# Low parts of a projection's weights on VectorE instead of GpSimd, in a hybrid attention and DeltaNet decoder step

## The chip, the core and the metric

The kernel runs on one core of a Trainium2 chip. The time is the device time of one execution in microseconds (us). Five engines work side by side, each through its own queue in order: TensorE (PE in the profile; its weight loads are PEld), VectorE (DVE), ScalarE (ACT), GpSimd (POOL) and SyncE (SP), which issues all DMA transfers here. An instruction that waits holds up all that stands behind it on its engine.

## The reference, cut to what matters

One layer of a decoder, for 1024 prompt tokens and 8 single-token samples, all in fp32:

```python
h = rms_norm(x, norm_mix_pre)
proj = h @ w_in                     # 1024 -> 2824 columns: q k v of attention, q k v z a b of DeltaNet
attn_o = window_attend(...)         # 8 heads, window 128, sinks, ALiBi
gdn_o  = gdn_chunked(...)           # 4 heads: conv, l2 norms, triangular inverse, scan over chunks
x = x + rms_norm(concat(attn_o, rms_norm(gdn_o) * silu(z)) @ w_out, norm_mix_post)
h = rms_norm(x, norm_ffn_pre)
x = x + rms_norm(relu(h @ w_up) ** 2 @ w_down, norm_ffn_post)
```

## The kernel before, in words

The tokens are worked in two halves, A (tokens 0 to 511 and the 8 samples) and B (512 to 1023). Every large product is made of three fp32r matmuls: an operand is split into a high part (a rounded copy, `wh` for weights, `h0h`, `h1h`, `xh` for activations) and a low part (the rest, `wl`, `h0l`, `h1l`, `xl`), and high times high, high times low and low times high are added up in PSUM.

The weights come in units: a block of 128 columns with 1024 rows, 512 KB. `w_dma` loads unit i into `wr` two units ahead, and `w_chain` splits it one unit ahead: ScalarE copies `wr` to `wh`, and then `wl = wr - wh` is made by VectorE or by GpSimd, or half by each. `wr`, `wh` and `wl` have two buffers each, so a unit can be split only when the unit two before it is done with. Unit 0 holds the two gate columns (a, b), units 1 to 22 the projections of half A, 23 the gates again, 24 to 41 the first 18 projections of half B, 42 to 49 the output projection `w_out` of half A, 50 to 53 the last four projections of half B, and from 54 on come the feed-forward weights. For units of the kind "pool" the planner decides from its own costs who makes `wl`: GpSimd if it is seen free early enough, half each if later, VectorE if later still. Units of the kind "dve" are VectorE's. Unit 1 is always GpSimd's, unit 2 always VectorE's.

The order of all instructions is not written by hand. While the program is built, the planner (`_Sched`) runs one main stream, the large matmuls, and many side chains (convolutions, gates, norms, attention heads, DeltaNet heads) as generators against a small cost table, and puts a step of a chain between the matmuls when the table says that its inputs are there. So a change in what one step costs, or in the engine that does it, shifts the order of everything that follows on all engines, until the chains have run out.

Side chains that matter below: the gate chain (`gates`), some 30 tiny VectorE instructions on the tile `abT` that end in `gg`, which TensorE multiplies with a triangle of ones into `gps` and transposes in `gtp`. The DeltaNet chain of a head: transposes `kps` and `qps`, products `kkq`, `Am`, an inversion on VectorE (`W`, `Ab`, `TW`), a round trip through DRAM (`Zd`), and then `yps`, `Y`, `zps`, `ztp` in three levels, and the scan `xps`, `ups`, `so`. After `w_out` each of half A's token tiles gets its residual and its norm: the sums of squares go to GpSimd (`ssA`), VectorE makes `hy` (residual) and `xrA` (normalised), and TensorE transposes that in `trp`, before the feed-forward can begin (matmuls into `two`). At the very end `run_tail` finishes the last product token tile by token tile, and `evac` writes the squares into a spare PSUM bank (`sq`).

Of the kernel before, what the change touches and what calls it, by code (L numbers as in the profile page):

```python
# [15 lines left out]
P = 128  # L16
DM = 1024
KD = DM // P
# [24 lines left out]
TH1, TH2 = 6500.0, 4500.0  # L43
# [219 lines left out]
def _body(ctx, tc, I, C, O):  # L263
    nc = tc.nc
    sp = nc.sync
    S = _Sched()
# [67 lines left out]
    def f32(ap):  # L334
        return ap.bitcast(F32)
# [55 lines left out]
    units = []  # L391
# [25 lines left out]
    def w_chain(i):  # L417
        _, shape, eng = units[i]
        raw, _, _, t, ev = wt[i]
        t0 = S.t["pe"]  # L420
        S.cur = max(S.t["pe"], t)
        yield
        if shape[-1] == 8:

            hi, lo = wt[i][1], None
            if hi is None:
                hi = wst_tile()
            CP(hi[:, :, 0:8], raw, "pool")
            TT(hi[:, :, 8:16], raw, f32(hi[:, :, 0:8]), ALU.subtract, "pool")
        else:  # L430
            hi = wp.tile([P] + shape, F32R, tag="wh", name="wh")
            lo = wp.tile([P] + shape, F32R, tag="wl", name="wl")
            A(hi, raw)
            yield
            n = 0 if i == 1 else shape[0] if i == 2 else shape[0] if eng == "dve" or max(S.t["pool"], S.cur) + 2300.0 > t0 + TH1 else (
                shape[0] // 2 if max(S.t["pool"], S.cur) + 2300.0 > t0 + TH2 else 0)
            c0 = S.cur
            if n:
                TT(lo[:, :n], raw[:, :n], f32(hi[:, :n]), ALU.subtract)
            c0, S.cur = S.cur, c0  # L440
            if n < shape[0]:
                TT(lo[:, n:], raw[:, n:], f32(hi[:, n:]), ALU.subtract, "pool")
            S.cur = max(S.cur, c0)
        wt[i][1:3] = [hi, lo]
        S.signal(ev)
# [1073 lines left out]
    LATE = 4  # L1519
# [3 lines left out]
            return [QO + 64 * h, QO + 64 * (4 + h)]  # L1523
        return [{"k": GO + 512, "q": GO, "v": GO + 1024, "z": ZO, "K": KO, "V": VO}[kd] + (h * P if kd in "kqvz" else 0)]

    def units_proj(g, cols):
        if cols[0][1] == 0:
            units.append(([(slice(None), w_in[:, :, ABO:ABO + 8])], [KD, 8], None))
        for kd, h in cols:
            cc_ = unit_cols(kd, h)  # L1530
            w = P // len(cc_)
            units.append(([((slice(None), slice(None), slice(i * w, (i + 1) * w)), w_in[:, :, c:c + w])
                           for i, c in enumerate(cc_)], [KD, P], "pool"))

    w_out = I["w_out"][0]
    KORD = [4, 0, 1, 5, 6, 7, 2, 3]
# [28 lines left out]
    units_proj(0, proj_cols(0))  # L1565
    units_proj(1, proj_cols(1)[:-LATE])
    units_w()
    units_proj(1, proj_cols(1)[-LATE:])
    PLAIN = (8, 2)
    units_up(PLAIN[0])  # L1570
    after_up = [len(units)]
# [9 lines left out]
    def unit_begin():  # L1581

        i = st["u"]
        st["u"] += 1
        return i
# [579 lines left out]
    class Contract:  # L2165
# [107 lines left out]
        def run_tail(self, i, bank, acc, dh):  # L2273
            unit_begin()
            xs = []

            for t, ks in ((0, (0, 1)), (1, (0, 1)), (0, (2, 3)), (1, (2, 3)), (2, range(4)), (3, range(4))):
                c = slice(t * P, (t + 1) * P)
                for k in ks:
                    u, j = i + k // 2, k % 2  # L2280
                    if k == len(xs):
                        yield from w_wait(u)
                        xs.append((yield from self.part(len(self.seq) - 4 + k)))
                    xh, xl = xs[k]
                    for ci, (a, w) in enumerate(((xh, 1), (xh, 2), (xl, 1))):
                        MM(acc[t], a[:, c], wt[u][w][:, j, :], False, k == 3 and ci == 2)
                        yield
                if k == 3:
                    S.cur = S.t["pe"] + S.LAT["pe"]
                    for _ in evac(acc[t], bank[t], P, self.ys[t], self.ss, t, dh, self.w, B.tile(t, [P, 512], "sq")):  # L2290
                        pass

    def evac(ps, bank, n, y, ss, i, dh, w, sq=None):
# [154 lines left out]
```

## Time and profile before

| | |
|---|---|
| time, median of 3 runs | 1304.32 us (1301.70 to 1306.08) |
| profiled execution, time | 1301.07 us |
| its span, first to last instruction | 1299.3 us |
| mean granted TensorE clock over the span | 0.993 of full speed |
| PE busy | 1261.0 us, 97% of the span |
| DVE busy | 902.4 us, 69% |
| ACT busy | 683.5 us, 53% |
| POOL busy | 357.2 us, 27% |

The profiled execution lies 1.8 us longer than its span, and 3.25 us below the median of the three runs. "Busy" is the time in which an engine has an instruction under way, with its waits for a port inside. For PE it says nothing on the clock: a matmul at half the clock is busy twice as long.

### The profile page before, as it was taken

The page shows a single profiled execution, that of the slowest core. Times are in us where ns is not written, and L with a number is a line of the kernel's source. Part 1 is how long each engine was busy: PE and PEld are TensorE (multiplying, and loading weights), DVE is VectorE, ACT ScalarE, POOL GpSimd, SP SyncE. Part 2 cuts the span into 40 slices and gives each one's busy share as a digit, 9 for nine tenths or more (in the row PEclk, how much of TensorE's full clock was granted, in tenths as well). Part 3 has the DMA queues.
Part 4 walks back from the last instruction along what each step waited for, and adds up shares of the span by engine and source line. Part 5 has one row for each costly group of instructions (what it writes and reads, how often), then busy time and mean ns, then how long its engine had stood idle before and what let it go on. Part 6 is the DMA issues. An engine that isn't in the chain of part 4 may idle for free.

```text
span 1299.3 us, 22677 instructions
## 1 busy us (share of the span) xinstructions
PE 1261.0 (97%) x8624; PEld 1081.0 (83%) x8624; DVE 902.4 (69%) x1708; ACT 683.5 (53%) x1409; POOL 357.2 (27%) x367
## 2 busy tenths in 40 slices
PE   8899999999999998999999999999998999999998
PEld 7898998777777776899999877777788999988886
DVE  5649878878777777678895479454478988544555
ACT  5466555645654545656665455343346666444442
POOL 4354344342253355103232330000034432000001
PEclk9899999999999998999999999999999999999999
DMA  6443325263233353133432443224345433243332
GB/s 184 131 118 100 79 66 139 75 149 89 65 100 94 94 159 119 51 112 105 114 111 98 130 162 99 81 82 149 93 121 155 119 100 103 92 162 98 97 98 98
DMA packets 199165, 142.57 MB, mean 110 GB/s; under 512 B 39406, under 2 KB 171822, under 8 KB 199032
## 3 DMA queue, kind: packets, MB, share of 16 engines
q1 hardware_dynamic: 199056, 141.12, 37.3%
q8 instruction: 68, 1.11, 0.4%
q14 instruction: 41, 0.34, 0.1%
HBM read 126.39 MB, written 15.85 MB: 109 GB/s over the span
## 4 chain that ended last, share of the span: by engine, by line
PE 84%; DVE 11%; ACT 2%; issue 1%; DMA 1%; POOL 1%; SPq 0%; DVEq 0%; POOLq 0%; ACTq 0%
PE acc L275 33%; PE ups L275 22%; PE pps L275 14%; PE dacc L275 2%; PE two L275 1%; DVE W L294 1%; PE so L275 1%; DVE kq L299 1%; PE kkq L275 1%; PE zps L275 1%; PE yps L275 1%; PE trp L282 1%; PE oa L275 1%; PE sps L275 1%; PE pps L282 1%
## 5 line engine op out<-in xcount | busy, mean ns | idle before, releaser
L275 PE MATMUL acc<-wh,xh 128*128 128x512 f32 x624 | 248.6, 398 | 0.0
L275 PE MATMUL acc<-wl,xh 128*128 128x512 f32 x624 | 245.0, 393 | 0.0
L275 PE MATMUL acc<-wh,xl 128*128 128x512 f32 x624 | 244.5, 392 | 0.1
L286 ACT ACTIVATE wh<-wr 128x1024 fp32r<-128x1024 f32 x161 | 169.2, 1051 | 67.1 <-PE pps L275 29.4
L294 DVE TENSOR_TENSOR xl<-u,xh 128x512 fp32r<-128x512 f32 x124 | 85.8, 692 | 143.1 <-ACT xh L286 143.1
L286 ACT ACTIVATE xh<-u 128x512 fp32r<-128x512 f32 x124 | 78.3, 631 | 191.7 <-PE acc L275 191.6
L294 POOL TENSOR_TENSOR wl<-wr,wh 128x1024 fp32r<-128x1024 f32 (+1 forms) x57 | 128.0, 2246 | 183.3 <-ACT wh L286 180.3
L294 DVE TENSOR_TENSOR wl<-wr,wh 128x1024 fp32r<-128x1024 f32 (+1 forms) x118 | 152.2, 1291 | 34.5 <-ACT wh L286 34.1
L275 PEld LDWEIGHTS acc<-wh,xh 128*128 128x128 f32 x624 | 117.1, 188 | 38.2 <-ACT xh L286 11.9
L275 PEld LDWEIGHTS acc<-wh,xl 128*128 128x128 f32 x624 | 117.2, 188 | 25.5 <-DVE xl L294 1.4
L294 POOL TENSOR_TENSOR st<-wr 128x512 f32<-128x512 f32 x54 | 85.4, 1588 | 189.5 <-DVE sl L294 84.0
L275 PEld LDWEIGHTS acc<-wl,xh 128*128 128x128 f32 x624 | 117.2, 188 | 22.8 <-DVE wl L294 0.2
L275 PE MATMUL ups<-T,sh 128*128 128x256 f32 (+1 forms) x648 | 120.6, 282 | 0.0
L275 PEld LDWEIGHTS ups<-T,sh 128*128 128x128 f32 x648 | 101.3, 188 | 0.0
L286 ACT ACTIVATE u<-u 128x520 f32<-128x520 f32 (+3 forms) x118 | 68.7, 582 | 53.8 <-DVE u L294 53.0
L275 PE MATMUL ups<-T,sl 128*128 128x256 f32 (+1 forms) x324 | 91.1, 281 | 0.3 <-DVE sl L294 0.3
L275 PE MATMUL ups<-h1h,wl 128*128 128x256 f32 (+2 forms) x328 | 86.5, 288 | 1.3 <-DVE wl L294 1.3
L275 PE MATMUL ups<-h1h,wh 128*128 128x256 f32 (+2 forms) x328 | 86.8, 288 | 0.0
L275 PE MATMUL ups<-h1l,wh 128*128 128x256 f32 (+2 forms) x328 | 86.6, 288 | 0.0
L275 PE MATMUL pps<-h1h,wl 128*128 128x512 f32 x176 | 73.1, 415 | 0.3 <-DVE wl L294 0.3
L275 PE MATMUL pps<-h1h,wh 128*128 128x512 f32 x176 | 72.0, 409 | 0.5 <-ACT acc L286 0.5
L275 PE MATMUL pps<-h1l,wh 128*128 128x512 f32 x176 | 72.1, 410 | 0.0
(403 smaller groups left out, 2876.8 us busy)
## 6 DMA issues: line engine op xcount, KB each, us to landing
wr<-in_w_up SPq DMA_DIRECT2D x64, 512.0 KB
wr<-in_w_down SPq DMA_DIRECT2D x64, 512.0 KB
wr<-in_w_in SPq DMA_DIRECT2D x36, 512.0 KB
wr<-in_w_in SPq DMA_DIRECT2D x16, 256.0 KB
wr<-in_w_out SPq DMA_DIRECT2D x16, 256.0 KB
wr<-in_w_out SPq DMA_DIRECT2D x32, 128.0 KB
xf<-x1d SPq DMA_DIRECT2D x8, 512.0 KB
xa<-in_x_prompt SPq DMA_DIRECT2D x4, 512.0 KB
```

The source lines that it names most:

```text
L275: ins = nc.tensor.matmul(out, lhsT=lhsT, rhs=rhs, start=start, stop=stop, **kw)
L282: ins = nc.tensor.transpose(out, in_, idn)
L286: ins = nc.scalar.activation(out, in_, func, **kw)
L294: ins = _e(eng).tensor_tensor(out=out, in0=a, in1=b, op=op)
L299: ins = nc.vector.scalar_tensor_tensor(out=out, in0=a, scalar=s, in1=b, op0=op0, op1=op1)
```

## The change

Three edits. The units with an index below 7, whose kind was "pool", get the kind "dve" (the special case of unit 2 goes away with that, and unit 1 stays with GpSimd). The last four projections of half B get the kind "dve" as well. In `run_tail` the squares of the third token tile go into bank 3 instead of 2, those of the fourth into bank 0 instead of 3.

```diff
@@ w_chain
-            n = 0 if i == 1 else shape[0] if i == 2 else shape[0] if eng == "dve" or max(S.t["pool"], S.cur) + 2300.0 > t0 + TH1 else (
+            n = 0 if i == 1 else shape[0] if eng == "dve" or max(S.t["pool"], S.cur) + 2300.0 > t0 + TH1 else (
                 shape[0] // 2 if max(S.t["pool"], S.cur) + 2300.0 > t0 + TH2 else 0)
@@
-    def units_proj(g, cols):
+    def units_proj(g, cols, eng="pool"):
...
-                           for i, c in enumerate(cc_)], [KD, P], "pool"))
+                           for i, c in enumerate(cc_)], [KD, P], "dve" if len(units) < 7 else eng))
...
-    units_proj(1, proj_cols(1)[-LATE:])
+    units_proj(1, proj_cols(1)[-LATE:], "dve")
@@ run_tail
-                    for _ in evac(acc[t], bank[t], P, self.ys[t], self.ss, t, dh, self.w, B.tile(t, [P, 512], "sq")):
+                    for _ in evac(acc[t], bank[t], P, self.ys[t], self.ss, t, dh, self.w, B.tile((0, 1, 3, 0)[t], [P, 512], "sq")):
```

The planner then makes another order on all five engines. Over the whole program the low part of 43 whole units and 14 half units was GpSimd's; now it is 34 whole and 16 half ones. TensorE's order is the same in its first 190 rows and again from row 2487 of 6798 on, which is the beginning of the feed-forward of half A. The two places below show how it shifts.

On VectorE, early in the projections of half A, this piece of the difference shows the low part of unit 3 coming in. `abT` rows belong to the gate chain and `kq` rows to the first convolution.

```order
 L294 TENSOR_TENSOR abT<-abT 128x5x4
 L308 TENSOR_SCALAR abT<-AB 128x5x4
+L294 TENSOR_TENSOR wl<-wr,wh 128x1024
 L299 SCALAR_TENSOR_TENSOR kq<-ext,cw,kq 128x4x128
 L306 TENSOR_SCALAR abT<-abT 128x5x4 x2
```

The low parts of units 4, 5 and 6 come in further on in the same way (those of 4 and 5 ahead of `gg`, that of 6 behind it), and three more rows of convolutions now stand ahead of `gg`: nine instead of six.

On TensorE, the place of `gps`, which needs `gg`. Before, it stands in the matmuls of unit 4 (`wh_475`, into `pps_557` and `pps_558`), four pairs after their start:

```order
L275 MATMUL pps_557<-h0h0_137,wl_476 128x256
L275 MATMUL pps_558<-h0h0_137,wl_476 128x264
L275 MATMUL pps_557<-h0h0_137,wh_475 128x256
L275 MATMUL pps_558<-h0h0_137,wh_475 128x264
L275 MATMUL gps_575<-gg_102,cst_sb_93 128x16
L275 MATMUL pps_557<-h0l0_139,wh_475 128x256
```

Now it stands at the end of unit 4, where unit 5 (`wh_551`) begins:

```order
L275 MATMUL pps_547<-h0h1_138,wl_476 128x256
L275 MATMUL pps_548<-h0h1_138,wl_476 128x264
L275 MATMUL gps_623<-gg_102,cst_sb_93 128x16
L275 MATMUL pps_629<-h0h0_137,wh_551 128x256
L275 MATMUL pps_630<-h0h0_137,wh_551 128x264
```

Counted from the first matmul of unit 2, `gps` came after 104 matmuls before and comes after 144 now.

On TensorE, in the last four projections of half B (units 50 to 53, 96 matmuls of 128x512 into `pps`), the first level of the last DeltaNet head. Before, it stands in the third of the four, after 71 of the 96 matmuls:

```order
L275 MATMUL pps_5708<-h1l1_902,wh_5644 128x512
L275 MATMUL yps_5773<-W_5109,Am1_5367 64x32 x8
L275 MATMUL pps_5708<-h1h1_900,wl_5645 128x512
L275 MATMUL pps_5790<-h1h0_899,wh_5710 128x512
L275 MATMUL pps_5790<-h1l0_901,wh_5710 128x512
L275 MATMUL zps_5796<-Y1_5772,T1_5730 64x32 x8
L275 MATMUL ztp_5797<-T1_5730,Y1_5772 64x32 x8
L275 MATMUL pps_5790<-h1h0_899,wl_5711 128x512
```

Now all 96 come first (`pps_5766` is the fourth projection), then the transposes of the normalised tokens with some attention scores (`sps`), and the head's first level behind them, with no large matmul between its steps:

```order
L275 MATMUL pps_5766<-h1h1_892,wl_5729 128x512
L282 MATMUL trp_5822<-ident_60,xrA_5582 128x128 x4
L282 MATMUL trp_5828<-ident_60,xrA_5582 128x128 x4
L282 MATMUL trp_5834<-ident_60,xrA_5582 128x128 x4
L275 MATMUL sps_5854<-KT_97,mix1_2044 128x256
L275 MATMUL sps_5855<-KT_97,mix1_2044 128x256
L282 MATMUL trp_5889<-ident_60,xrA_5582 128x128 x4
L275 MATMUL yps_5896<-W_5170,Am1_5417 64x32 x8
L275 MATMUL zps_5915<-Y1_5895,T1_5872 64x32 x8
L275 MATMUL ztp_5916<-T1_5872,Y1_5895 64x32 x8
L282 MATMUL trp_5937<-ident_60,xrA_5582 128x128 x4
L275 MATMUL two_5953<-h1h0_5815,wh_5768 128x256
```

On VectorE the end of that head's inversion (the copy of `TW` that goes to DRAM) now stands right behind the `xrA` of the third token tile; before, it stood ahead of the residual of the second tile.

## Rows read from the trace of the kernel before

**Rows 1.** Stretches: length; PE, PEld, DVE, ACT, POOL busy us (instructions); clock, DMA, GB/s
```profile
0.00:555.00 555.00, 529.29 (x4068) 444.73 (x4069) 407.63 (x1053) 302.17 (x764) 224.87 (x255) 0.99 0.39 106
555.00:1299.30 744.30, 731.68 (x4558) 636.29 (x4557) 494.75 (x656) 381.29 (x646) 132.38 (x112) 1.00 0.37 112
0.00:20.00 20.00, 14.47 (x69) 10.74 (x70) 10.48 (x22) 12.60 (x26) 10.46 (x25) 1.00 0.82 229
```

**Rows 2.** Waits of PE: who for whom, us in total, times, longest
```profile
PE zps L275 <- DVE Y L294: 4.2, 1, 4.2
PE gps L275 <- DVE gg L299: 3.9, 1, 3.9
```

**Rows 3.** Busy times (PE, PEld, DVE, ACT, POOL) and clock around `gps`
```profile
27.60:39.84 12.24, 12.24 (x105) 12.24 (x103) 9.74 (x26) 5.58 (x10) 6.30 (x8) 1.00 0.76 213
39.84:44.12 4.28, 0.40 (x5) 0.19 (x3) 4.18 (x9) 0.85 (x3) 2.67 (x3) 0.89 0.03 9
44.12:49.90 5.78, 5.78 (x26) 5.71 (x27) 3.83 (x7) 1.35 (x3) 0.00 (x0) 0.50 0.05 13
```

**Rows 4.** Busy times and clock in the last four projections of half B
```profile
473.00:497.00 24.00, 20.22 (x107) 15.58 (x106) 20.68 (x23) 12.23 (x23) 18.90 (x22) 1.00 0.79 246
492.00:505.00 13.00, 7.13 (x64) 5.53 (x63) 11.59 (x14) 5.57 (x11) 10.92 (x13) 0.74 0.54 169
```

**Rows 5.** Timeline of PE there: start, duration, operation, [idle before it]
```profile
473.68 0.50 PE L275 MATMUL pps<-h1h,wh 128*128 128x512 f32 x1 [0.52 <-ACT acc L286]
...
493.91 0.66 PE L275 MATMUL yps<-W,Am 64*64 64x32 f32 x16 [1.71 <-DMA W<-Zd]
...
499.61 1.06 PE L275 MATMUL zps<-Y,T 64*64 64x32 f32 x16 [4.15 <-DVE Y L294]
...
512.59 1.97 PE L282 MATMUL trp<-ident,xrA 128*128 128x128 f32 x16
...
517.15 2.10 PE L275 MATMUL sps<-KT,mix 64*128 64x256 f32 x16
```

**Rows 6.** Timeline of POOL (start, duration, operation, [idle before it]), one of three such
```profile
34.45 2.40 POOL L294 TENSOR_TENSOR wl<-wr,wh 128x1024 fp32r<-128x1024 f32 x1 [2.23 <-ACT wh L286]
```

**Rows 7.** Timeline of DVE ahead of `gps`
```profile
29.77 2.40 DVE L299 SCALAR_TENSOR_TENSOR kq<-ext,cw,kq 128x512 f32<-128x512 f32 x1 [2.06 <-ACT kq L286]
32.69 0.65 DVE L299 SCALAR_TENSOR_TENSOR kq<-ext,cw,kq 128x512 f32<-128x512 f32 x1
...
34.50 2.38 DVE L294 TENSOR_TENSOR abT<-abT 128x20 f32<-128x20 f32 x1
...
43.88 0.18 DVE L299 SCALAR_TENSOR_TENSOR gg<-abT,alg 128x20 f32<-128x20 f32 x1
```

**Rows 8.** Groups of the page: low parts on either engine, whole span
```profile
L294 POOL TENSOR_TENSOR wl<-wr,wh 128x1024 fp32r<-128x1024 f32 (+1 forms) x57 | 128.0, 2246 | 183.3 <-ACT wh L286 180.3
L294 DVE TENSOR_TENSOR wl<-wr,wh 128x1024 fp32r<-128x1024 f32 (+1 forms) x118 | 152.2, 1291 | 34.5 <-ACT wh L286 34.1
```

**Rows 9.** Timeline of ACT, the high part of unit 5
```profile
39.08 1.06 ACT L286 ACTIVATE wh<-wr 128x1024 fp32r<-128x1024 f32 x1 [3.02 <-PE pps L275]
```

**Rows 10.** Timeline of POOL in the last four projections of half B
```profile
495.13 2.35 POOL L294 TENSOR_TENSOR wl<-wr,wh 128x1024 fp32r<-128x1024 f32 x1
```

**Rows 11.** Timeline of DVE in the last four projections of half B
```profile
477.98 1.78 DVE L294 TENSOR_TENSOR wl<-wr,wh 128x512 fp32r<-128x512 f32 x1
...
495.20 3.35 DVE L299 SCALAR_TENSOR_TENSOR hy<-hy,ssA,xrA 128x1024 f32<-128x1024 f32 x1 [0.72 <-POOL ssA L294]
...
499.66 1.28 DVE L299 SCALAR_TENSOR_TENSOR xrA<-hy,ssA 128x1024 f32<-128x1024 f32 x1
```

**Rows 12.** Timeline of an earlier head: end of its inversion, its `yps`
```profile
383.08 0.67 DVE L323 TENSOR_REDUCE TW<-W 32x64 f32<-32x512 f32 x1
...
390.61 0.66 PE L275 MATMUL yps<-W,Am 64*64 64x32 f32 x16 [0.36 <-DMA W<-Zd]
```

**Rows 13.** Timeline of ACT in the tail, squares of the third token tile
```profile
1290.20 0.58 ACT L286 ACTIVATE sq<-acc 128x512 f32<-128x512 f32 x1 [2.03 <-PE acc L275]
```

## The prediction

> **What bounds the kernel now.** I read the busy times by stretch first. TensorE is busy for 529.3 of the first 555 us and for 731.7 of the other 744.3 [rows 1], and its order from the feed-forward of half A on is unchanged, so what the change can win or lose lies in the first 555 us: 25.7 us of TensorE's idle time, and the matmuls that run at the lower clock. 5.5 us of that idle time is the start of the kernel [rows 1], ahead of all that changes. The waits of TensorE [rows 2] name the two longest, 3.9 us before `gps` and 4.2 us before `zps`, and each is a single wait. They lie at the two places that the change touches; call them A (us 40 to 50) and B (us 492 to 505).
>
> At A TensorE is full and at full clock until 39.84, then it works 0.40 of 4.28 us, and the next 5.78 us run at a granted clock of 0.50, which is 1.2 GHz of 2.4 [rows 3]. So A costs 3.88 us of waiting and half of 5.78, 2.9 us, together 6.8. At B TensorE works 7.13 of 13 us at a mean clock of 0.74 [rows 4]: 5.87 us idle, which is the 1.71 before `yps` and the 4.15 before `zps` [rows 5], and 13 x 0.26 / 0.5 = 6.8 us at the lower level, part of them idle. At most half of 6.8 is lost to it, 3.4; I take 2 as my estimate. B costs about 8. The rest, 25.7 - 5.5 - 3.9 - 5.9 = 10.4 us, is spread over 500 us in waits of which none is as long.
>
> **Place A.** The reader should see why `gg` is late. While GpSimd makes a low part from 34.45 to 36.85 [rows 6], VectorE's `abT` instruction on 20 columns runs from 34.50 to 36.88 [rows 7]: it ends when GpSimd does. The first tap `kq` takes 2.40 us beside such a low part and 0.65 without [rows 7]. Three low parts fall into this chain, so they cost VectorE about 1.75 + 2.2 + 2.2 = 6.1 us, and the planner's table has no such cost. With the change these low parts are VectorE's own, at no more than the 1.29 us mean of its group [rows 8]: three of them ahead of `gg`, 3.9 us. Three more convolution rows stand ahead of it, 3 x 0.65 = 2.0. `gg`, which ended at 43.88 + 0.18 = 44.06 [rows 7], would end at 44.06 - 6.1 + 3.9 + 2.0 = 43.9. VectorE must also wait for the high parts in this order; that of unit 5 is done at 39.08 + 1.06 = 40.1 [rows 9], and by my sum VectorE gets there at about the same time, so I allow 0.5 more: 44.4.
>
> TensorE used to stand at `gps` at 40.24. The new place is 40 matmuls later, 0.117 us each (105 in 12.24, [rows 3]), 4.7 us: 44.9. So `gg` should be there with half a microsecond to spare, the wait goes, and with it the fall of the clock, which came after it. Cover for the low parts themselves: the low part of unit 5 is done at 40.1 + 1.29 = 41.4 and needed at 44.9; if VectorE were more than 3.5 us later than that, each microsecond more would be one of TensorE's. A short wait at `gtp` may be left, since one convolution row now lies between `gps` and the copy that `gtp` reads. Gain at A: between 3.9 (the clock still falls, 2.9 lost again) and 6.8; I take 6.5, since the cause is removed and not moved.
>
> The Trainium skill has a rule on this (SBUF — State Buffer, Who interferes with whom): a VectorE instruction with two SBUF inputs and a GpSimd instruction that reads SBUF cannot run together, and the later one is blocked for the whole of the other. The trace agrees, 2.38 us for a 20-column instruction. But another page of the Trainium skill, Perfetto Trace Analysis, Optimizing Scalar/DVE Operations, says that moving work between these two engines might not help for that reason, and taken alone that speaks against the change. By it VectorE is taken for about as long either way, and the sum would be zero.
>
> **Place B.** Here the reader should compare what is late. GpSimd's low part at 495.13 [rows 10] lies beside the residual `hy` of 3.35 us at 495.20, against 1.28 for the same size [rows 11]; I found one more such pair, so 2 x 2.07 = 4.1 us of VectorE go. In their place come four whole low parts, 4 x 1.29 = 5.2, less the 1.78 of the half one that VectorE already made there [rows 11], so 3.4 more. The start of the inversion of the last head, about 2.3 us of small instructions by my estimate, now also falls into this stretch. Before, the `xrA` of the third token tile ended at 499.66 + 1.28 = 500.94 [rows 11], 27.3 us after the first of the 96 matmuls at 473.68 [rows 5]. Now: 27.3 + 3.4 + 2.3 - 4.1 = 28.9 if VectorE had no other slack; but it had 24 - 20.68 = 3.3 us idle [rows 4], some of it in waits for GpSimd, so 25.6 to 28.9. Middle: 27.
>
> TensorE: before, the 71 matmuls up to `yps` and four small groups of transposes took 493.91 - 473.68 - 1.71 = 18.5 us [rows 5], 0.26 each; 96 take 25.0, and two transposes of 0.49 (1.97 for four, [rows 5]) 1.0. It then waits for the third tile from 26 to 27. From there to `yps` it has five transposes, 2.5, and a group of scores, half of 2.10 [rows 5]: 3.5 us. But `yps` needs the round trip through DRAM, and at an earlier head it took 390.61 - (383.08 + 0.67) = 6.9 us from the last reduction to `yps` [rows 12]. That reduction, 0.7 us, now stands right behind the third `xrA`, so `yps` waits 0.7 + 6.9 - 3.5 = 4.1 us, with nothing left to put before it. `zps` follows with no large matmul between and waits for `Y`, one small VectorE instruction and the way there and back; I estimate 0.9, and 2 if VectorE is behind. Sum: 1 + 4.1 + 0.9 = 6.0 idle, against 5.87 before, and a clock that falls again for about as long. So B is exchanged for itself: 0, with bounds from +3 (third tile at once, clock stays up) to -4 (third tile 2 us later still, `Y` late, clock lost 3.4).
>
> **The tail.** The squares of the third token tile begin at 1290.20 [rows 13], and the trace puts the idle time before them to the last matmul of that tile alone; no bank held them up. The fourth writes into a bank that nobody reads. I cost this edit at 0; a matmul, not the bank, is the cover.
>
> **The middle.** From A to B the order of some 2,000 rows is shuffled. GpSimd has nine whole low parts less (2.25 us mean of all forms, [rows 8]) and VectorE nine more; the planner knows what a low part costs on VectorE and not what it costs beside GpSimd, so its places should be no worse. I count 0, with 4 us either way out of the 10.4 that wait there.
>
> **Sum.** 6.5 + 0 + 0 + 0. Against the profiled execution, 1301.07 - 6.5 = 1294.6. The median of the runs lies 3.25 above that execution, so the prediction is 1304.32 - 6.5 = 1297.8 us.
>
> **The rivals.** A difference of 0.3%, 3.9 us, is about what a measurement of this kernel can tell from none.
>
> First, A goes and B shrinks too: VectorE delivers the third tile on time and the shuffle is kind. 6.8 + 3 + up to 4 gives 1304.3 - 13.8 = 1290.5. For it speaks that GpSimd's sums of squares no longer stand behind its low parts; against it the round trip, which no engine's speed shortens. Chance 0.19.
>
> Second, the wait only moves: A's gain is eaten by a new wait in the shuffled middle, one of 3 to 4 us, as two already are, with the clock down behind it. 6.5 - 4 - 2 leaves about 1304, within 0.3%. For it speaks that VectorE, the busier of the two (407.6 against 224.9 us of 555, [rows 1]), takes on more. The sentence of the Trainium skill against moving work between the two (Perfetto Trace Analysis, Optimizing Scalar/DVE Operations) would end here too. Chance 0.24.
>
> Third, slower: VectorE becomes the bound at B. TensorE's loss there is then the wait for the third tile, 4.1 before `yps`, 2 before `zps`, and 4 to 5 to the clock. If the tile came 36 us after the first of the 96 matmuls instead of 27, that is 10 + 4.1 + 2 + 4.5 = 20.6 against 8 before: 12.6 lost, less A's 6.5, 1304.3 + 6 = 1310. It eats A's gain from about 30 us on and makes the kernel measurably slower from 34, or from 31 if A keeps its slow clock and gains 3.9 alone. For it speaks that VectorE is busy 20.68 of 24 us there [rows 4]; against it that a fifth of this is time at the port, which goes. Chance 0.12.
>
> **How the numbers follow.** My forecast, A gone and B exchanged, has 0.45, and with the first rival faster has 0.64; same 0.24, slower 0.12. The range takes in the first rival's 1290 and the upper end of no change: 1304.3 and the spread of the runs, 1306. Below and above lie about 0.2. The likeliest case's own range is 1294 to 1300.
>
> **What would show it.** In the profile after: no wait of TensorE before `gps`, and a full clock from us 40 to 50; no VectorE instruction of 2.4 us from 27 to 45. At B a wait before `yps` put down to the DMA of `W`, of about 4 us, and a short one before `zps`; the third tile's `trp` some 27 us after the first of the 96 matmuls. TensorE's idle time of the first 555 us near 22, and everything behind the first `ups` shifted as a block. The prediction is wrong if a new wait of over 3 us with a fall of the clock stands between A and B, or if the low parts of units 3 to 6 hold up TensorE themselves.

## The result, and the profile after

The changed kernel is slower: 1312.99 us (median of six runs, 1310.95 to 1317.48) against 1304.30 for the kernel before in the same comparison (six runs, 1300.94 to 1306.13). The ratio is 1.0074, with a 95% interval of 1.0055 to 1.0092. The profiled execution took 1312.95 us, its span 1311.2, its mean granted clock 0.988.

The time was not lost where the change was made. Starts of TensorE's first matmul at seven places, and the end of the span, from the two timelines (us):

| place in the program | before | after | difference |
|---|---|---|---|
| `gps` of half A (place A) | 44.12 | 44.35 | +0.2 |
| first projection of half B | 209.93 | 203.66 | -6.3 |
| `gps` of half B | 249.01 | 250.47 | +1.5 |
| second `dkr` (decode states) | 284.85 | 292.06 | +7.2 |
| first `acc` (`w_out` of half A) | 402.05 | 409.15 | +7.1 |
| first of the last four projections (place B) | 473.68 | 485.14 | +11.5 |
| first `two` (feed-forward of half A) | 516.50 | 522.35 | +5.9 |
| end of the span | 1299.3 | 1311.2 | +11.9 |

So A gave 6 us, as forecast. The stretch from half B's first projection to the second `dkr`, which the prediction counted as 0, cost 13.5. From the first `acc` on, B's 5.6 are mostly work brought forward: TensorE is busy 5.3 us longer in the stretch ahead of the last four projections (69.67 and 74.95 us) and 3.4 less in them (36.74 and 33.33), so the two together gained 1.3. TensorE's order is that of before again from us 554.8 before and 563.1 after. There the changed kernel is 8.3 us late, about what the medians differ by (8.7). The other 3.5 us of the 11.9 come behind that, nearly all at one `ups` of the feed-forward of half B, where two executions of one and the same order differ as well (see the experiment on SP below); the profiled execution of before lies 3.25 below its median and that of after on it.

Place A in the profile after, timeline of VectorE (start, duration, operation): a low part, a tap that took 2.40 us before [rows 7], and `gg`.

```profile
28.63 1.22 DVE L294 TENSOR_TENSOR wl<-wr,wh 128x1024 fp32r<-128x1024 f32 x1 [1.45 <-ACT wh L286]
29.77 0.74 DVE L299 SCALAR_TENSOR_TENSOR kq<-ext,cw,kq 128x512 f32<-128x512 f32 x1
...
42.84 0.18 DVE L299 SCALAR_TENSOR_TENSOR gg<-abT,alg 128x20 f32<-128x20 f32 x1
```

`gg` ends at 43.02 and `gps` starts at 44.35 with no wait. The waits of TensorE after (who for whom, us in total, times, longest) name what came instead; [rows 2] has those of before:

```profile
PE dkr L275 <- DMA S<-in_state_gdn: 4.8, 2, 4.2
PE gps L275 <- DVE gg L299: 3.7, 1, 3.7
...
PE xps L275 <- DVE S L299: 2.6, 2, 2.0
PE pps L275 <- DVE wl L294: 2.5, 3, 1.3
```

This `gps` is that of half B. Busy times by stretch after (length; PE, PEld, DVE, ACT, POOL busy; clock, DMA, GB/s), to be read beside [rows 1, 3]:

```profile
0.00:555.00 555.00, 523.89 (x3999) 438.36 (x4000) 406.43 (x1059) 298.25 (x755) 206.44 (x244) 0.98 0.39 105
40.00:49.90 9.90, 9.90 (x85) 9.88 (x84) 7.09 (x17) 3.52 (x8) 0.77 (x2) 1.00 0.35 76
200.00:240.00 40.00, 36.93 (x301) 28.27 (x300) 32.20 (x141) 20.49 (x70) 13.02 (x24) 0.96 0.43 112
240.00:260.00 20.00, 16.34 (x118) 12.74 (x117) 16.39 (x41) 7.58 (x19) 7.03 (x5) 0.83 0.17 47
280.00:300.00 20.00, 14.56 (x117) 11.43 (x117) 8.17 (x24) 4.40 (x13) 8.50 (x7) 0.83 0.65 160
```

And the same three stretches of the middle before:

```profile
200.00:240.00 40.00, 40.00 (x322) 30.94 (x321) 33.06 (x130) 24.09 (x71) 13.72 (x28) 1.00 0.52 129
240.00:260.00 20.00, 19.87 (x165) 15.32 (x164) 18.48 (x65) 12.01 (x37) 8.71 (x8) 1.00 0.21 54
280.00:300.00 20.00, 19.63 (x167) 15.98 (x166) 11.02 (x38) 9.31 (x27) 6.61 (x6) 1.00 0.50 131
```

At A TensorE is full at full clock. In the middle two stretches of 20 us, all but full before, now idle 3.7 and 5.4 us and run at 0.83 of the clock. VectorE is not busier there than before (16.39 against 18.48, 8.17 against 11.02), so it is late and not overloaded.

**The first wait.** VectorE at the gates of half B, then GpSimd beside it, after:

```profile
241.96 2.00 DVE L294 TENSOR_TENSOR abT<-abT 128x16 f32<-128x16 f32 x1
...
246.66 1.80 DVE L299 SCALAR_TENSOR_TENSOR abT<-abT 128x16 f32<-128x16 f32 x1
248.50 1.82 DVE L299 SCALAR_TENSOR_TENSOR gg<-abT,alg 128x16 f32<-128x16 f32 x1
```

```profile
241.55 2.38 POOL L294 TENSOR_TENSOR wl<-wr,wh 128x1024 fp32r<-128x1024 f32 x1 [5.86 <-ACT wh L286]
...
246.54 3.75 POOL L294 TENSOR_TENSOR S<-S,dec 128x1024 f32<-128x1024 f32 x2 [2.44 <-ACT kq L286]
```

The last two instructions of the chain, 0.17 us each before, each end with one of GpSimd's two scalings of the decode states. It is what the prediction found at A, with another GpSimd instruction. Before, the scalings came behind `gg`:

```profile
247.63 0.17 DVE L299 SCALAR_TENSOR_TENSOR gg<-abT,alg 128x16 f32<-128x16 f32 x1
```

```profile
250.81 5.34 POOL L294 TENSOR_TENSOR S<-S,dec 128x1024 f32<-128x1024 f32 x2 [8.24 <-issue]
```

**The second wait.** The queue of SP, then VectorE's last write of the state and a low part of its own, GpSimd, and TensorE, after:

```profile
281.93 0.99 SPq L328 DMA_DIRECT2D wr<-in_w_in  x2
282.97 0.89 SPq L328 DMA_DIRECT2D out_s_gdn<-S  x1
287.68 0.99 SPq L328 DMA_DIRECT2D S<-in_state_gdn  x2
```

```profile
277.42 1.13 DVE L299 SCALAR_TENSOR_TENSOR S<-ubp,dec,S 128x128 f32<-128x128 f32 x4 [1.08 <-PE ubp L282]
278.46 1.22 DVE L294 TENSOR_TENSOR wl<-wr,wh 128x1024 fp32r<-128x1024 f32 x1
...
278.84 3.06 POOL L294 TENSOR_TENSOR wl<-wr,wh 128x1024 fp32r<-128x1024 f32 x1 [3.81 <-ACT wh L286]
...
292.06 1.08 PE L275 MATMUL dkr<-S,dec 128*32 128x128 f32 x16 [4.24 <-DMA S<-in_state_gdn]
```

The state is ready at 278.55, but SP stands at the load of unit 31, whose buffer is free only when GpSimd has made a low part at 281.90. The write goes out 4.4 us late, and the load into the same buffer, and with it `dkr`, behind it. Before, write and load went out as follows, and `dkr` had no wait:

```profile
274.42 0.38 SPq L328 DMA_DIRECT2D out_s_gdn<-S  x1
277.66 0.99 SPq L328 DMA_DIRECT2D S<-in_state_gdn  x2
```

### The profile page after: what moved, and what is told of

It is laid out like the page before. It is cut to its first block, busy times and chain, and to the rows that moved or that the text cites. A ratio compares the mean times of both kernels' runs of the same rounds, so it can differ in the third digit from the quotient of the medians.

```text
span 1311.2 us, 22688 instructions
## 1 busy us (share of the span) xinstructions
PE 1266.9 (97%) x8624; PEld 1085.3 (83%) x8624; DVE 905.9 (69%) x1719; ACT 684.5 (52%) x1409; POOL 339.6 (26%) x358
## 4 chain that ended last, share of the span: by engine, by line
PE 83%; DVE 10%; DMA 2%; ACT 2%; POOL 1%; issue 1%; SPq 0%; DVEq 0%; POOLq 0%; ACTq 0%
PE acc L275 34%; PE ups L275 22%; PE pps L275 14%; PE dacc L275 2%; PE two L275 2%; PE so L275 1%; PE trp L282 1%; PE oa L275 1%; PE zps L275 1%; PE yps L275 1%; PE pps L282 1%; DVE wl L294 1%; DVE kq L299 1%; PE sps L275 1%; DVE vT L299 1%
## 5 line engine op out<-in xcount | busy, mean ns | idle before, releaser
L294 DVE TENSOR_TENSOR wl<-wr,wh 128x1024 fp32r<-128x1024 f32 (+1 forms) x129 | 166.8, 1294 | 35.8 <-ACT wh L286 35.1
L294 POOL TENSOR_TENSOR wl<-wr,wh 128x1024 fp32r<-128x1024 f32 (+1 forms) x48 | 106.4, 2216 | 172.5 <-ACT wh L286 171.9
L275 PEld LDWEIGHTS acc<-wh,xh 128*128 128x128 f32 x624 | 117.1, 188 | 38.5 <-ACT xh L286 11.9
```

Of the source, the lines that this page charges most:

```text
L275: ins = nc.tensor.matmul(out, lhsT=lhsT, rhs=rhs, start=start, stop=stop, **kw)
L294: ins = _e(eng).tensor_tensor(out=out, in0=a, in1=b, op=op)
```

## The experiments

**Theory 1:** the loss is made by the order that the planner writes for the middle once units 3 to 6 have moved; (1a) a GpSimd instruction beside the gate chain, (1b) the second load of states, each with the clock down behind it. **Rivals:** the load on VectorE whatever the order; place B; a loss that is spread so that no single wait matters. A unit's "booked" cost is the planner's, which sets the order; the engine that does the work can be chosen apart from it. Each median is set against the runs of the kernel before on the same chip.

**The first edit alone.**

```diff
-            n = 0 if i == 1 else shape[0] if i == 2 else shape[0] if eng == "dve" or ...
+            n = 0 if i == 1 else shape[0] if eng == "dve" or ...
-                           for i, c in enumerate(cc_)], [KD, P], "pool"))
+                           for i, c in enumerate(cc_)], [KD, P], "dve" if len(units) < 7 else "pool"))
```

> The first edit alone: units 3 to 6 are VectorE's, the last four projections of half B and the tail's banks are as before. Theory 1 (the order of the middle): the loss is made by the order that the planner writes once units 3 to 6 have moved, at the gates of half B (a wait of 3.7 us in the changed kernel) and at the second state load (4.2 us), each with the clock down behind it. Then this kernel has all of the loss, 17.5 us between A and B, and A's gain of 6, but not the 5.6 us that the changed kernel won at B: 1313.0 + 5.6 = 1318, at least 1313. Rival (place B): the four projections on VectorE lose the time; then this kernel keeps A's gain, 1304.3 - 6 = 1298.

Measured 1316.20 against 1303.33: 12.9 us slower, ratio 1.0102 (1.0080 to 1.0123). Both waits are there, 3.7 and 4.0, with the clock at 0.91 in us 240 to 260 and 0.83 in 280 to 300. Its longest wait is a third one, at place B, with the clock at 0.50 in us 508 to 516:

```profile
508.20 1.12 PE L282 MATMUL vps<-ident,vT 128*128 128x128 f32 x4 [6.13 <-DVE vT L299]
```

That is about what B cost before (5.9 us of waits); in the changed kernel this wait is 0.8.

**The second and third edit alone** (no run has the second without the third).

```diff
-    units_proj(1, proj_cols(1)[-LATE:])
+    units_proj(1, proj_cols(1)[-LATE:], "dve")
-... B.tile(t, [P, 512], "sq")
+... B.tile((0, 1, 3, 0)[t], [P, 512], "sq")
```

> The second and third edit alone: the last four projections of half B are VectorE's and the squares of the tail go into banks 0, 1, 3, 0; units 3 to 6 are as before, so the order stands as before until shortly ahead of those projections. Theory 1: B wins the 5.6 us that it won in the changed kernel and nothing is lost ahead of it: 1304.3 - 5.6 = 1298.7, with A's wait of 3.9 us before gps still there. Rival (place B): slower than before, 1309 or more.

Measured 1299.40 against 1303.33: 3.9 us faster, ratio 0.9971 (0.9952 to 0.9990). Place B is not the loss.

**The third edit alone** (the second line of the last diff).

> The third edit alone: the squares of the third and fourth token tile of the tail go into banks 3 and 0, all else is before. The prediction's step (the tail costs nothing: a matmul, not the bank, holds those squares): 1303.5, within 0.3%. Rival: a bank held the tail up and the 8.7 us are made of other parts than thought: a difference of over 3 us either way.

Measured 1304.03 against 1303.16, ratio 1.0007 (0.9994 to 1.0020): nothing, so the 3.9 are put down to the second edit. Within the intervals the parts add up: 12.9 - 3.9 = 9.0, for 8.7 measured.

**The engine without the order.**

```diff
+                if 2 < i < 7:
+                    nc.vector.tensor_tensor(out=lo[:, n:], in0=raw[:, n:], in1=f32(hi[:, n:]), op=ALU.subtract)
+                    S.op("pool", 2.1 * n_of(lo[:, n:]) + 150, None)
+                else:
                     TT(lo[:, n:], raw[:, n:], f32(hi[:, n:]), ALU.subtract, "pool")
```

> The engine without the order: the low parts of units 3 to 6 are issued on VectorE, but the planner books them on GpSimd as before, so every engine's order is that of before except that these instructions stand on VectorE. Theory 1: nothing is lost in the middle. At A gps stands 40 matmuls earlier than in the changed kernel, so gg, at 44.06 - 6.1 + 3.9 = 41.9 by the sum of the prediction, is still some 1.6 us late: a gain of 2 to 6, so 1298 to 1302. Rival 2 (VectorE's load): the low parts make VectorE late behind A whatever the order, and the waits of 3 to 4 us in the middle come here too: 1308 or more.

Measured 1297.33 against 1303.33: 6.0 us faster, ratio 0.9951 (0.9934 to 0.9968). Its stretches (columns as above):

```profile
40.00:50.00 10.00, 10.00 (x85) 9.98 (x85) 6.90 (x12) 6.20 (x15) 2.63 (x3) 1.00 0.54 120
...
240.00:260.00 20.00, 18.37 (x147) 14.09 (x146) 19.18 (x49) 12.47 (x34) 9.52 (x8) 1.00 0.31 71
280.00:300.00 20.00, 19.63 (x119) 16.35 (x118) 14.08 (x50) 10.88 (x32) 5.62 (x7) 1.00 0.44 117
```

`gg` is in time even at the earlier place of `gps` (no wait; the expectation had 1.6 us of it, with three low parts ahead of `gg`, where this order has two), and the middle has neither of the two waits. The edit by itself is worth 6.0; with the planner's new order it costs 12.9. The order is worth 18.9. To that order belong the engines that the planner chooses for the other units: GpSimd makes 34 whole and 18 half low parts in the kernel with the first edit alone, 39 and 14 here.

**The order without the engine.**

```diff
+                if 2 < i < 7:
+                    nc.gpsimd.tensor_tensor(out=lo[:, :n], in0=raw[:, :n], in1=f32(hi[:, :n]), op=ALU.subtract)
+                    S.op("dve", n_of(lo[:, :n]) / 0.96 + 70, None)
+                else:
                     TT(lo[:, :n], raw[:, :n], f32(hi[:, :n]), ALU.subtract)
```

> The order without the engine: all orders are those of the changed kernel, but the low parts of units 3 to 6 are issued on GpSimd at the places where the changed kernel has them on VectorE. Theory 1: the middle's loss stays, since the two waits lie 200 us behind these instructions and are made by the order: the waits of about 3.7 us before half B's gps and 4.2 us before the second dkr are there, and A gives back some of its gain: 1313 to 1318. Rival 2 (VectorE's load): with VectorE relieved the middle's waits go, 1304 or less.

Measured 1314.48 against 1303.33, ratio 1.0084 (1.0060 to 1.0109): the loss stays with VectorE relieved, and both waits do (3.7 and 3.9). The rival of VectorE's load falls.

**The two waits, one at a time, in the changed kernel.** Without GpSimd's scaling:

```diff
-                TT(S0[:, j], S0[:, j], bc(dgb[:, 1, n:n + 8].unsqueeze(2), [P, NB, P]), ALU.mult, "pool")
+                S.op("pool", 2.1 * n_of(S0[:, j]) + 150, None)
```

> The changed kernel without GpSimd's scaling of the decode states (S<-S,dec, four instructions of 128x1024 in all; the planner still books them, so all orders stay). It leaves out that scaling, so the states that it writes are not scaled. Theory 1a (the port): two of the four run beside the last two instructions of half B's gate chain, abT of 1.80 us and gg of 1.82 us against 0.17 each alone, so gg comes 1.63 + 1.65 = 3.3 us earlier, the wait of 3.7 us before half B's gps falls to 0.4, and the granted clock of 0.83 in us 240 to 260 goes back to 1.00, for at most 3.4 us: 1313.0 - 3.3 to - 6.7, so 1306 to 1310. Rival (the place alone): the chain is late by its place in the order whatever GpSimd does; then the wait stays and so does the time, 1313.

Without the second load:

```diff
-                S0 = load_S0(1)
-                S.cur = dd["t"]
+                for j in range(2):
+                    keep = S.cur
+                    S.dma(4 * P * n_of(S0[:, j]))
+                    dd["t"], S.cur = S.cur, keep
+                S.cur = dd["t"]
```

> The changed kernel without the second load of decode states (S<-in_state_gdn, two transfers; the planner still books them, so all orders stay). It leaves out the second pair of heads' states and works on the first pair's again. Theory 1b (the transfer): the second dkr waits 4.2 us for that load, which stands on SP behind two loads of weights and the write of the first states, and a second 0.5; without it both waits go and the granted clock of 0.83 in us 280 to 300 goes back to 1.00: 1313.0 - 4.8 to - 8.2, so 1305 to 1308. Rival (late anyway): the arithmetic ahead of dkr is as late as the load, or the attention and DeltaNet heads behind it swallow the gain: 1311 to 1313.

Without either (both diffs):

> The changed kernel without the scaling and without the second load (left out as in the two kernels of one each; all orders stay). Theory 1a and 1b together: these two waits and the clock behind them are most of what the middle lost, so the gains add up: 1313.0 minus the sum of the two gains, 8 to 13, so 1300 to 1305. Rival (one hides the other, or a third wait takes over): the sum is 3 us or more short of the two single gains.

Against before's 1303.60 of that chip they gave 1307.64 (+4.0, ratio 1.0038, 1.0025 to 1.0052), 1304.55 (+1.0, 1.0019, 1.0004 to 1.0034) and 1300.14 (-3.5, 0.9979, 0.9968 to 0.9990). From the changed kernel's +8.7 that is 4.7, 7.7 and 12.2: within the intervals the two add up. Without the scaling `gg` ends 1.3 us behind the start of the first `dkr`, 4.6 in the changed kernel, and the wait before `gps` is 0.4. The end of the gate chain reads:

```profile
248.99 0.17 DVE L299 SCALAR_TENSOR_TENSOR abT<-abT 128x16 f32<-128x16 f32 x1
249.20 0.18 DVE L299 SCALAR_TENSOR_TENSOR gg<-abT,alg 128x16 f32<-128x16 f32 x1
```

and without either the two stretches are

```profile
240.00:260.00 20.00, 19.61 (x146) 15.42 (x145) 17.93 (x49) 12.72 (x30) 6.59 (x8) 1.00 0.23 60
280.00:300.00 20.00, 20.00 (x154) 17.36 (x152) 10.39 (x38) 10.92 (x30) 7.05 (x6) 1.00 0.44 116
```

Idle time and clock come back together. All three kernels leave work out, so they show what the waits cost and not a way to save it. Without either, the stretch from half B's first projection to the second `dkr` is 77.9 us, against 74.9 before; the 3 us that are left are about what two shorter waits at us 204 to 208 take, `pps` 1.3 and `abp` 1.8, which all three traces keep.

**Two neighbours on SP exchanged** (all work done).

```diff
+            if i == 31:
+                S.dma(4 * P * n_of(raw[sl]))
+                t, S.cur = S.cur, S.t["pe"]
+                late.append((raw[sl], src))
+            else:
+                t = D(raw[sl], src)
...
                 D(O["s_gdn"][0, :, 2 * hp_ + j].rearrange("b d e -> d b e"), S0[:, j])
+            while late:
+                o, src = late.pop()
+                sp.dma_start(out=o, in_=src)
```

> The changed kernel with two neighbours on SP exchanged: the write of the second decode state (out_s_gdn) now stands ahead of the load of unit 31's weights instead of behind it; every other row of every engine is that of the changed kernel, and nothing is left out. Theory 1b, refined (the queue): the state was ready at 278.55, but SP stood at unit 31's load until GpSimd had made the low part of unit 29 at 281.90 and wrote the state only at 282.97; the second load of states waits for that write. With the exchange write and load move up by some 4.4 us, the waits of 4.2 and 0.5 us before the second dkr go and so does the lower clock behind them: 1313.0 - 4.8 to - 8.2, like the kernel without the load (1304.55). Rival (the transfer itself): the write and the load need their time, the load comes at most 1 us earlier: 1311 to 1313.

> The kernel with the two rows of SP exchanged once more, for a second profile. If a fall of the clock behind the rest of the wait before the second dkr (2.2 us) comes in some executions and not in others, the profile is either like the first (1303.6, clock 1.00 in us 280 to 300) or some 5 to 10 us longer with the granted clock below 0.9 in us 280 to 300, and the same elsewhere. If the difference lies elsewhere, the windows show it there.

Its first profiled execution took 1303.6 us, the second 1308.1; the median was 1309.94 against 1303.16 (six runs, 1303.6 to 1315.5), ratio 1.0069 (1.0047 to 1.0091). SP in the first profile:

```profile
276.26 0.38 SPq L328 DMA_DIRECT2D out_s_gdn<-S  x1
279.61 1.01 SPq L1505 DMA_DIRECT2D wr<-in_w_in  x2
280.72 1.69 SPq L328 DMA_DIRECT2D S<-in_state_gdn  x2
```

The write now goes out with the last state. From the first `dkr` to the second half of the second one, which needs the second of the two transfers, it is 48.0 us in the changed kernel, and 44.0 and 43.9 in the two profiles; the waits fall from 4.8 to 2.6 and 2.5, and the clock in us 280 to 300 is 1.00 in both. So the queue was the cause of about half of that wait. What makes the rest isn't shown: it can be the transfer, or the load of unit 31, right behind which the load of the states still goes out. But the gain of 4 us at the place is not seen in the median, whose interval overlaps the changed kernel's.

The two profiles, of one order, differ by 4.5 us, and not in us 280 to 300. They part at us 145, where VectorE's tap `vT` meets a low part of GpSimd. VectorE and GpSimd in the first profile:

```profile
145.40 0.73 DVE L299 SCALAR_TENSOR_TENSOR vT<-ext,cw,vT 128x512 f32<-128x512 f32 x1
```

```profile
144.65 3.74 POOL L294 TENSOR_TENSOR wl<-wr,wh 128x1024 fp32r<-128x1024 f32 x1 [3.16 <-ACT wh L286]
```

and in the second:

```profile
145.27 2.85 DVE L299 SCALAR_TENSOR_TENSOR vT<-ext,cw,vT 128x512 f32<-128x512 f32 x1
```

```profile
144.54 3.04 POOL L294 TENSOR_TENSOR wl<-wr,wh 128x1024 fp32r<-128x1024 f32 x1 [3.16 <-ACT wh L286]
```

In the second alone TensorE then waits 2.0 us before `xps`, and its clock is 0.66 in us 150 to 155. Half B begins at 201.5 and 205.1; 2.2 us of this are left at the second `dkr`. The other 2.4 come at an `ups` in the feed-forward of half B, near us 985, where the wait is 1.1 in the first and 2.1 in the second, with the clock down behind it. The five executions of 1309.5 us and more have no profile, so where they lose the rest stays open.

**With the scaling on ScalarE as well** (all work done).

```diff
-                TT(S0[:, j], S0[:, j], bc(dgb[:, 1, n:n + 8].unsqueeze(2), [P, NB, P]), ALU.mult, "pool")
+                for b in range(NB):
+                    nc.scalar.activation(S0[:, j, b], S0[:, j, b], AF.Copy, scale=dgb[:, 1, n + b:n + b + 1])
+                S.op("pool", 2.1 * n_of(S0[:, j]) + 150, None)
```

> The changed kernel with the two rows of SP exchanged, and with the scaling of the decode states on ScalarE (16 small instructions for each two of GpSimd's; booked as before, so the order of everything else stays); nothing is left out. Theory 1a and 1b: the gate chain of half B runs beside no GpSimd instruction of two SBUF inputs and gg is on time, the second dkr waits 2 us or less: the gain of the kernel without the scaling, 5.4, adds to the 3.1 of the exchange: 1304.5, or less where the clock stays up, down to the 1300.1 of the kernel that leaves both out. Rival (a new wait): ScalarE's 16 instructions stand ahead of evacuations that TensorE waits for, and the gain of the scaling is lost: 1308 to 1310.

Measured 1311.69 against 1303.00, ratio 1.0071 (1.0057 to 1.0085): the rival, a little above its range. The wait before half B's `gps` falls to 0.4, and a new one stands behind the second scaling, ScalarE's row and TensorE's:

```profile
292.11 4.78 ACT L1490 ACTIVATE S<-S,dec 128x128 f32<-128x128 f32 x16
...
297.10 0.80 PE L275 MATMUL so<-ut,kd 128*128 128x128 f32 x2 [2.45 <-ACT ut L286]
```

with a clock of 0.74 in us 280 to 300. Again an instruction stands ahead of one that TensorE waits for, now on ScalarE. So no kernel that does all the work won the loss back at these two places; what they cost is shown only by the kernels that leave work out.

**Other draws of the order.** Theory 2: the middle is a draw, so another price in the planner's table, with units 3 to 6 and the last four projections on VectorE as in the changed kernel, gives another result. (The planner chooses the engines of the other units anew each time: GpSimd makes 30 to 35 whole and 13 to 16 half low parts in these draws.) The number added is 150, 400, -400 or 250 ns:

```diff
                 TT(lo[:, :n], raw[:, :n], f32(hi[:, :n]), ALU.subtract)
+                if 2 < i < 7:
+                    S.t["dve"] += 150.0
+                    S.cur += 150.0
```

> The changed kernel with one number of the planner's table changed: a low part of units 3 to 6 on VectorE is booked at 150 ns more, 1.29 us, which is what the trace shows for one. The engines of all low parts of units 0 to 6 stay, the order is drawn anew, and now half B's gps stands 21 matmul groups ahead of the first dkr, as before, instead of one behind it. Theory 2 (a draw): what the middle loses hangs on where the gate chain falls, not on the engine; GpSimd's scaling of the states comes behind dkr and so misses the gate chain: no wait of over 1 us before half B's gps, and 1294 to 1304. Rival (systematic): the planner's order with these units on VectorE loses about 9 us however it is drawn: 1310 to 1316.

> As the kernel booked at 1.29 us, with 400 ns more instead of 150 (1.54 us). In this draw half B's gps stands one matmul group behind the first dkr, as in the changed kernel. Theory 2 (a draw): GpSimd's scaling of the states falls beside the end of the gate chain again: a wait of 2 to 4 us before half B's gps with a lower clock behind it, and 1303 to 1312. Rival (systematic): 1310 to 1316, as for the other draw; a wait before gps in both draws or in neither speaks against the place of dkr as the cause.

> A third draw: a low part of units 3 to 6 is booked 400 ns below the changed kernel, at 0.74 us; engines as in the changed kernel. Theory 2 (a draw): anything from 1294 to 1313, and the long waits of the changed kernel in the middle (3.7 before half B's gps, 4.2 before the second dkr) stand only in draws of 1306 and more. Rival (systematic): 1309 to 1316.

> A fourth draw: a low part of units 3 to 6 is booked 250 ns above the changed kernel, at 1.39 us, 0.1 above the draw that gave 1296; engines as in the changed kernel. Theory 2 (a draw): 1294 to 1313, and no nearer to 1296 for lying near it in the table. Rival (a right price helps): a table near the measured 1.29 us gives good orders: 1294 to 1300, while the third draw, far from it, is slower.

| low part of units 3 to 6 booked at | median, us | of before, us | ratio (95%) |
|---|---|---|---|
| 0.74 us | 1295.11 | 1303.00 | 0.9951 (0.9934 to 0.9968) |
| 1.14 us (the changed kernel) | 1312.99 | 1304.30 | 1.0074 (1.0055 to 1.0092) |
| 1.29 us | 1296.09 | 1303.16 | 0.9952 (0.9934 to 0.9969) |
| 1.39 us | 1302.59 | 1303.00 | 1.0003 (0.9991 to 1.0015) |
| 1.54 us | 1309.41 | 1303.16 | 1.0060 (1.0037 to 1.0082) |

Theory 2 holds: the same change is a gain of 8 us, nothing, or a loss of 9. The right price does not help: one of these low parts takes 1.2 us in the traces (the 1.29 is a mean of whole and half ones), the two draws nearest to that, at 1.14 and 1.29, give a loss of 8.7 and a gain of 7.1, and 0.74 is as good as 1.29. The rule for which draws are bad failed too: the draw at 1.54 has `dkr` ahead of half B's `gps`, and no wait there. It loses at other places, among them one wait of 4.3 (of the 5.1) and one of 2.3:

```profile
PE otp L282 <- DVE kq L294: 5.1, 2, 4.3
PE ups L275 <- DVE sl L294: 2.6, 2, 2.3
```

The second stands near us 590, in the feed-forward, where TensorE's order is that of before already. Against the profile of before, the profiled execution of this draw (1313.6 us) loses 6.7 us there and 4.8 ahead of it: what a draw loses need not lie in the middle.

**Both edits of the engine without the first one's order** (the diffs of the engine without the order and of the second and third edit).

> Both edits of the engine, without the order that the first one makes: units 3 to 6 are booked on GpSimd as before and issued on VectorE, the last four projections are VectorE's for planner and chip, and the banks of the tail are 0, 1, 3, 0. Theory 1: the gains of the two places add up, 6.0 at A by the kernel with the engine moved alone and 3.9 at B by the kernel with the last four projections alone: 1303.3 - 9.9 = 1293.4. Rival (no sum): the head and the token tiles at B come 6 us earlier and meet the same round trips and weights, so B gives nothing more: 1297.3.

Measured 1294.70 against 1303.60: 8.9 us faster, ratio 0.9937 (0.9917 to 0.9958), for 9.9 expected. The interval, 5.5 to 10.8 us, takes in the rival's 6.0 too. Two of the draws and the engine without the order can't be told apart from it by their intervals.

## Why the prediction was wrong

**What bounds the kernel: right.** Of the 11.9 us between the two profiles 8.3 have come by us 563, in TensorE's waits and the clock behind them; its idle time of the first 555 us is 31.1, where 22 was forecast. That nothing can be lost behind it does not hold for every order: the draw at 1.54 us lost 6.7 there.

**Place A, 6.5 us: right,** in size and cause. `gg` came at 43.0 for 44.4 forecast, the low parts took 1.2 us for 1.29 (a mean of whole and half ones; the whole ones of before take 1.36), no VectorE instruction of 2.4 us is left from us 27 to 45, and the engine alone gave 6.0, without the later place of `gps` that the prediction counted on. The rule of the Trainium skill (SBUF — State Buffer, Who interferes with whom), that a VectorE instruction with two SBUF inputs and a GpSimd instruction that reads SBUF exclude each other, is borne out again at half B's gates: 1.82 us beside the scaling, 0.18 without it. The sentence of the Trainium skill that moving work between the two might not help (Perfetto Trace Analysis, Optimizing Scalar/DVE Operations) is not: with the order held, it helped by 6.0.

**Place B, 0 with +3 and -4: mis-sized,** at 3.9 gained alone (1.3 to 6.3). The third tile came 511.81 - 485.14 = 26.7 us after the first of the 96 matmuls (27 forecast). The wait of 4.1 before `yps` did not come, since more was put before it than the prediction's 3.5 us:

```profile
511.81 0.63 PE L282 MATMUL trp<-ident,xrA 128*128 128x128 f32 x4 [0.72 <-DVE xrA L299]
...
516.71 2.82 PE L282 MATMUL trp<-ident,xrA 128*128 128x128 f32 x12 [0.96 <-DVE sm L312]
519.46 0.75 PE L275 MATMUL yps<-W,Am 64*64 64x32 f32 x16
520.74 0.66 PE L275 MATMUL zps<-Y,T 64*64 64x32 f32 x16 [0.53 <-DVE Y L294]
```

From the third tile's transposes to `yps` it is 7.7 us, which covers the round trip; [rows 5] has the waits of before. From the first of the 96 matmuls to the first `two` TensorE idles 3.9 us, where 6.0 were forecast. With the second and third edit alone `yps` and `zps` have no wait either; 1.9 before `vps` and 1.8 before `trp` stand there, for 5.9 before.

**The tail, 0: right** (ratio 1.0007).

**The middle, "I count 0, with 4 us either way": the step that failed.** It measured 13.5 us lost. Its reason, that the planner's "places should be no worse", was no estimate of a size. The 4 us were taken out of the 10.4 that TensorE waited there before, as if a new order could only trade the waits that there were; but those 10.4 were what one good order had left. The changed kernel's own draw made two new waits of about 4 us, each with the fall of the clock that the prediction itself had priced at A (2.9 us), and some shorter ones; the first edit's order as a whole cost 18.9. The rows of before held half of the warning: the port, a price that the planner's table lacks, had made A's wait, and it holds for every chain that meets GpSimd. To SP's queue, which made about half of the second wait, the prediction gives no price in the middle. The prediction's count is off too: by the trace, GpSimd makes 32 whole and 16 half low parts in the changed kernel, eleven whole ones less than before and not nine; VectorE makes nine whole and two half ones more. Part of that is the planner's own new choice.

**The rivals.** The second (the wait only moves into the middle, with the clock down) was the mechanism, and the prediction's last sentence names it; its price, one wait of 4 and 2 for the clock, was less than half of what came. The third gave nearly the right time, 1310, by a wrong mechanism: VectorE did not become the bound at B. The range to 1306 was too narrow by the same term.

## What to carry to other kernels

Where a program orders the instructions by a cost table, a change of one cost or engine is two changes: the engine, which can be priced from the rows, and a new order, whose price is a draw. Here the engines were worth 8.9 us (5.5 to 10.8) with the order held, and the five orders drawn with them took back between 1.0 and 17.6 of it, so hold the order while you change the engine, or draw several orders and keep the best, before you judge the idea. A chain of tiny instructions that ends in a matmul, and a queue in which one transfer waits for a buffer, were the two places in the changed kernel's order; the draw at 1.54 us lost at others, so a new order has to be read from its own profile.

## What was not expected of the hardware

Executions of one kernel with one order differ by more than the kernel before led to expect: 12 us (1303.6 to 1315.5) with the two rows exchanged, against 5 to 8 for before; the shortest had a mean clock of 0.993 and the longest 0.986. Part of this is decided where VectorE and GpSimd meet: in two executions of one order it was GpSimd's low part that took longer (3.74 us, the tap 0.73) or VectorE's tap (2.85 us, the low part 3.04). Nor does the length of a wait alone tell what the clock does. A wait of 2.0 us before `xps` came with 0.66 in us 150 to 155 in the second profile of the exchange, and with 1.00 in the changed kernel's; a wait of 2.2 us before `dkr` left the clock at 1.00 in us 280 to 300 in both profiles of the exchange; waits of 3.2 there (the kernel without the scaling) and 4.2 came with 0.80 and 0.83. And the exclusion costs GpSimd too: the low part at 278.84, which began while VectorE was at one of its own, took 3.06 us, that at 241.55 2.38.
